# Two-layer decoder trunk: the first weights in halves, one queue for the first columns of x, later transposes in TensorE's order

## The chip, the cores and the metric

The kernel runs on one core of a Trainium2 chip. The metric is device time in microseconds (us) from start to end of one launch. Before the change, three runs took 282.30, 281.93 and 282.25 us; the median is 282.25 us. A profiled execution of the same program took 281.82 us; the first to the last instruction of it span 280.0 us.

Engines are named as in the profile: PE is TensorE's matmul stream, PEld its weight loads, DVE is VectorE, ACT ScalarE, POOL GpSimd, SP SyncE. SP computes nothing here: it issues nearly all DMAs, in the order of its program, and waits where one of them must wait.

## The reference, cut to what matters

Sequence 256, model width 1024, two layers, heads of 64. Each layer projects the normalised rows to ten column blocks, runs three kinds of attention on them, gates each with silu, and multiplies by one output matrix. A last norm follows.

```python
for layer in range(DEPTH):
    h = rms_norm(x, norm_g[layer])
    proj = jnp.einsum('btd,dc->btc', h, w_in[layer])
    sb_q, sb_k, sb_v, sb_g, mb_q, mb_k, mb_v, mb_g, mem_q, mem_g = jnp.split(proj, split_at, axis=-1)
    o_sb = stick_breaking_attention(...)          # 6 heads, causal, in log space
    o_sb = merge_heads(o_sb) * jax.nn.silu(sb_g)
    o_mb = moba_attention(q_mb, k_mb, ...)        # 6 heads, rotary, causal softmax (one block here)
    o_mb = merge_heads(o_mb) * jax.nn.silu(mb_g)
    m = rms_norm(mem, mem_norm_g[layer])
    mk, mv = jnp.split(jnp.einsum('bmd,dc->bmc', m, w_mem_kv[layer]), 2, axis=-1)
    o_mem = memory_attention(..., mk, mv)         # 4 heads, softmax over 256 memory tokens
    o_mem = merge_heads(o_mem) * jax.nn.silu(mem_g)
    mixed = jnp.concatenate([o_sb, o_mb, o_mem], axis=-1)
    x = x + jnp.einsum('btc,cd->btd', mixed, w_out[layer])
return rms_norm(x, final_norm_g)
```

## The kernel before, in words

**Products in three passes.** Each factor of a projection is split into a rounded part (hi) and the rest (lo); TensorE computes hi times hi, hi times lo and lo times hi. For weights, a transfer brings a chunk of 384 KB (128 partitions by 768 numbers) into one of five buffers `raw`; ScalarE or VectorE casts it to hi (tile `hl`, line 245 or 266), VectorE subtracts to get lo (line 251). There are seven `hl` buffers, so the weights can run some chunks ahead of TensorE. When VectorE has finished the lo of a chunk, its `raw` buffer is free and SP issues the load of the chunk five places later. A chunk holds as many of the eight slices of the contraction (k = 0 to 7, called rows of weights here) as fit into 768 columns.

**The start.** Layer 0 begins with `sb_qk`: 768 columns, so one chunk is one row of weights. Row k needs the transposed input x^T of that row too (tile `uT`, 128 KB a row), which ScalarE scales to hi and VectorE to lo (tile `T`, lines 247 and 255). The first row of weights comes as two chunks of 384 columns, the others as one each. ACT's queue issues the two halves of row 0 and row 1 of x^T, SP's queue the rest. Six banks of PSUM accumulate the six blocks of 128 columns side by side; row 0 is computed first for banks 1 to 3 (first half of the weights) and then for banks 4 to 6.

**The order of the work.** All engines get their instructions in an order that the program works out while it is built: tasks (generators) ask for an engine, for marks that must be set, and for buffers; the class `Sched` keeps a clock for each engine from estimated costs, and at each step takes the request that can start first, with priorities among those that can start at nearly the same time. The large projections are one task, `main`, with the lowest priority; scores, transposes and products with values are tasks that slip in between. The pieces of weights are loaded and multiplied in the order of the table `ORDER`. TensorE's order is fixed once the program is built: an instruction whose data is late holds up all behind it.

**Between the layers.** When the output projection of layer 0 ends, the norm of layer 1 is computed for two tiles of 128 rows: squares, logarithm and exponential on ScalarE, two products of 512 columns per tile on VectorE (tile `w`, line 255), four transposes for each on TensorE (line 234, from `w` and the identity in `cst`), and hi and lo of the result into `T` (lines 245 and 251). TensorE has the memory projections `mk` and `mv` of layer 1 to do at that time; they don't need the norm.

**Turns through memory.** The softmax weights of a pair of heads and the rotated keys are transposed in blocks on VectorE (tile `D`), written to memory and read back in another order (tile `Z`): two DMAs one after the other, for which the planner counts a latency `TRIP_LAT` each on top of its transfer time.

Lines that the steps of the prediction touch: the costs and places in lines 27 to 52, `_avail` (119 to 141), the cutting into chunks (370 to 385), `hi_task` (404 to 411), the first loads (436 to 444), `norm_task` (570 to 592), `soft_head` (709 to 734), and the loop of `sb_qk` in `main` (from line 1050).

Of the kernel before, what the change touches and what calls it, by code (L numbers as in the profile page):

```python
# [27 lines left out]
RAW = 5  # L28
KORD = (0, 1, 2, 3, 4, 5, 6, 7)
LAT_SAME, LAT_CROSS = 130.0, 240.0  # L30
P_H0 = -8
P_RX = 1
P_M0 = 12
P_RM = 12
P_M1 = 4
URG = 2
X67_AT = 6
CST_AT = 7
X0_AT = 9
X1_AT = 12  # L40
DMA_GBS = 380.0
SP_ISSUE = 450.0
DMA_LAT = 2200.0
DMA_GBS_1K = 300.0
TRIP_LAT = 4000.0
MEM_FIRST = (False, False)
MEM_AT = 1
ORDER = (["sb_qk", "mem_q", "mb_k", "mb_q", "mk", "mv", "sb_v", "sb_g", "mb_g", "mb_v", "mem_g"],
         ["mk", "mv", "sb_g", "mb_k", "mb_q", "mb_g", "mem_g", "sb_q", "mem_q", "sb_k", "sb_v", "mb_v"])
GATES = {"sb_g": ((0, 1, 2),), "mb_g": ((0, 1, 2),), "mem_g": ((0,), (1,))}  # L50
HOLD = 4000.0
SPARE2 = 2
DVE_HI = 400.0
# [27 lines left out]
class Sched:  # L81
# [37 lines left out]
    def _avail(self, k, eng):  # L119
        r = k.req  # L120
        t = k.t
        if k.eng == eng:
            t += 0.0 if eng == "pe" else LAT_SAME
        elif k.eng:
            t += LAT_CROSS
        for n in r.get("need", ()):
            if n not in self.ready:
                return None
            t = max(t, self.ready[n])
        for tag in r.get("alloc", ()):  # L130
            items = self.res[tag].items
            spare = r.get("spare", 0)
            if "form" in r and r["form"] == self.form:
                spare = r.get("spare2", spare)
            if len(items) <= spare:
                return None
            t = max(t, self.res[tag].best()[0])
        cond = r.get("cond")
        if cond is not None and not cond():
            return None  # L140
        return t

    def _by_form(self, cands):

# [54 lines left out]
def hybrid_trunk(ctx: ExitStack, tc: tile.TileContext, x, mem, norm_g, w_in, w_mem_kv, w_out,  # L199
                 final_norm_g, xT, memT, gcols, consts, out):  # L200
    nc = tc.nc
# [67 lines left out]
    def R(*eng, **kw):  # L269
        kw["eng"] = [e if isinstance(e, tuple) else (e, 0.0) for e in eng]  # L270
        return kw
# [81 lines left out]
    for l in range(DEPTH):  # L353
# [4 lines left out]
        for n in names:  # L358
            if n in COLS:
                c, w = COLS[n]  # L360
                order.append(Piece(n, l, wi[:, :, c:c + w], w))
            elif n[:2] == "wo":
                c = 384 * int(n[2])
                w = min(384, D - c)
# [5 lines left out]
    chunks = []  # L370
    for p in order:
        i = 0
        while i < KT:
            kk = [p.kord[i]]
            i += 1
            while i < KT and len(kk) < p.nk and p.kord[i] == kk[-1] + 1:
                kk.append(p.kord[i])
                i += 1
            half = p.width // 2 if not chunks else p.width
            for c in range(0, p.width, half):  # L380
                for n, k in enumerate(kk):
                    p.kmap.setdefault(k, []).append((c, len(chunks), n * half))
                chunks.append((p, kk, c, half))
# [20 lines left out]
    def hi_task():  # L404
        for j, (p, kk, _, w) in enumerate(chunks):
            w = len(kk) * w
            e, _ = yield R(*([] if j == 0 else [("act", 0.833 * w)]), ("dve", 0.52 * w + DVE_HI), 
                           need=[("raw", j)] + ([("free", j - LEAD)] if j >= LEAD else []))
            copy(his[j % LEAD][:, :w], raws[j % RAW][:, :w], e)
            S.mark(("hi", j))  # L410
            prog["hi"] = j + 1
# [24 lines left out]
    dma_chunk(q=nc.scalar)  # L436
    load_xT(0, 1)
    dma_chunk(q=nc.scalar)
    load_xT(1, 2, nc.scalar)
    for k in range(2, 4):  # L440
        dma_chunk()
        load_xT(k, k + 1)
    dma_chunk()
    load_xT(4, 6)

    def bcast_row(vec, name):
# [123 lines left out]
    def norm_task(l, t, H, done):  # L570
        src = xs[:, t, :]
        r = ss[l, t][:, 7:8]
        yield from rstd(ss[l, t], 3, r)
        for q in range(2):
            s = slice(q * 512, (q + 1) * 512)
            _, (w,) = yield R("dve", need=[("gb", 0)], alloc=["w"])
            stt(w, src[:, s], r, gb[:, s], OP.mult, OP.mult)
            _, (pt,) = yield R("pe", alloc=["bank"])
            for i in range(4):
                tr(pt[:, i * 128:(i + 1) * 128], w[:, i * 128:(i + 1) * 128], ident)  # L580
            S.free("w", w)
            pv = pt.rearrange("p (k c) -> p k c", k=4)
            o_hi = H[0][:, q * 4:q * 4 + 4, t * 128:(t + 1) * 128]
            o_lo = H[1][:, q * 4:q * 4 + 4, t * 128:(t + 1) * 128]
            yield R("act")
            act(o_hi, pv)
            yield R("dve")
            tt(o_lo, pv, o_hi.bitcast(F32), OP.subtract)
            S.free("bank", pt)
            S.mark(done + (q,))  # L590
        S.mark(done)
# [22 lines left out]


    wTs, scs, sps, ws, Fs, ropes = {}, {}, {}, {}, {}, {}
    turn = {"sb": 0, "w": 0}
    HCOL = {"sb": 0, "mb": 384, "mem": 768}
    VN = {"sb": "sb_v", "mb": "mb_v", "mem": "mv"}

# [14 lines left out]
    def pair_scores(l, kind, c):  # L635
# [20 lines left out]
        if kind != "mem":  # L656
            yield R("pe")
            for h in range(2):
                for j, o in enumerate((slice(0, 128), slice(256, 384))):
                    if kind == "sb":  # L660
                        mm(sc[h][:, o], masks[:, 0, :], identb, False, j == 1)
                    else:
                        mm(sc[h][:, o], identb, masks[:, 1, :], False, j == 1)
        for h in range(2):
            S.mark(("qkdone", l, kind, 2 * c + h))
            scs[l, kind, 2 * c + h] = sc[h]
# [41 lines left out]

    def soft_head(l, h, kind):
        mb = kind == "mb"  # L710
        first = (2 if mb else 0) if MEM_FIRST[l] else (0 if mb else 3)
        reg = [(0, 128), (128, 384)] if mb else [(0, 256), (256, 512)]
        _, (st,) = yield R("dve", alloc=["st"], need=[("qkdone", l, kind, h)])
        sc = scs.pop((l, kind, h))
        for t, (r0, r1) in enumerate(reg):
            nc.vector.tensor_reduce(st[:, t:t + 1], sc[:, r0:r1], axis=AX.X, op=OP.max, negate=True)  # L716
            S.op("dve", 1.0417 * (r1 - r0) + 65.0)
            if t == 0:
                yield R("dve")
        _, (w,) = yield R("act", alloc=["w"], cond=lambda: 5 * l + first + h // 2 <= turn["w"] + 1)  # L720
        for t, (r0, r1) in enumerate(reg):
            act(w[:, r0:r1], sc[:, r0:r1], AF.Exp, bias=st[:, t:t + 1], accum_out=st[:, 2 + t:3 + t])
        S.free("bank", sc)
        yield R("dve")
        nc.vector.reciprocal(st[:, 0:2], st[:, 2:4])
        S.op("dve", 81.0)
        yield R("dve")
        for t, (r0, r1) in enumerate(reg):
            ts(w[:, r0:r1], w[:, r0:r1], st[:, t:t + 1])
        S.free("st", st)  # L730
        S.mark(("w", l, kind, h))
        ws[l, kind, h] = w
# [244 lines left out]
    def main():  # L977
# [26 lines left out]
        for l in range(DEPTH):  # L1004
# [45 lines left out]
            if l == 0:  # L1050
# [3 lines left out]
                    accs.append((yield from bank()))  # L1054
                for k in range(KT):
                    if k < 4:
                        groups = [range(3), range(3, 6)] if k == 0 else [range(6)]
                        for g in groups:
                            j, o = p.loc(k, g[0] * 128)
                            o -= g[0] * 128  # L1060
# [129 lines left out]
```

## Time and profile before

| | us |
|---|---|
| runs | 282.30, 281.93, 282.25 (median 282.25) |
| profiled execution | 281.82 |
| its span | 280.0 |
| PE busy | 270.7 (97% of the span) |
| PEld busy | 242.7 (87%) |
| DVE busy | 229.9 (82%) |
| ACT busy | 185.0 (66%) |
| POOL busy | 3.9 (1%) |
| mean granted TensorE clock | 0.998 of full speed |

An engine's busy time is the time covered by its instructions. PE's records overlap, since matmuls are pipelined, so a PE that is always busy need not run at its peak; what the tables of waits show is time in which no record covers PE. An instruction is listed with the tile it writes, an arrow, and the tiles it reads; "T<-uT,gc" is a slice of x^T being scaled.

### The profile page before, as it was taken

How to read it: one execution, taken by the hardware profiler on the slowest of the kernel's cores; microseconds unless marked ns; L12 is line 12 of the kernel's file. 1: busy time of each engine (PE TensorE's matmuls, PEld its weight loads, DVE VectorE, ACT ScalarE, POOL GpSimd, SP SyncE). 2: the span in 40 equal slices, each digit the busy share in tenths (PEclk: the TensorE clock that was granted, in tenths of full speed). 3: DMA queues.
4: the chain of work that ended last, by engine and by line, in shares of the span. 5: the costliest groups of instructions: out<-in, count | busy, mean ns of one | idle time of the engine just before them, and what ended most of it. 6: DMA issues, size and time to landing. Idle time of an engine off the chain costs nothing.

```text
span 280.0 us, 4979 instructions
## 1 busy us (share of the span) xinstructions
PE 270.7 (97%) x1713; PEld 242.7 (87%) x1713; DVE 229.9 (82%) x514; ACT 185.0 (66%) x414; POOL 3.9 (1%) x10
## 2 busy tenths in 40 slices
PE   7899999999999999999999999999999999999991
PEld 4788999898888898898978899988888898988991
DVE  3789899998999999995889489739999999994273
ACT  3879799984696787771866384648974898433053
POOL 0030000010000000000000000000000000000000
PEclk9999999999999999999999999999999999999999
DMA  6999938697588998885476846857358988890004
GB/s 218 348 385 367 367 103 259 188 246 285 165 267 212 263 314 250 242 210 167 129 248 199 272 147 208 250 167 218 104 148 290 248 265 219 263 248 14 0 0 150
DMA packets 45720, 60.49 MB, mean 216 GB/s; under 512 B 3328, under 2 KB 42368, under 8 KB 45696
## 3 DMA queue, kind: packets, MB, share of 16 engines
q1 hardware_dynamic: 44688, 58.22, 67.7%
q0 software_dynamic: 288, 1.05, 1.5%
q10 hardware_dynamic: 720, 0.92, 1.0%
q8 instruction: 13, 0.21, 0.3%
q14 instruction: 11, 0.09, 0.1%
HBM read 53.89 MB, written 6.29 MB: 215 GB/s over the span
## 4 chain that ended last, share of the span: by engine, by line
PE 91%; DMA 4%; ACT 2%; DVE 2%; issue 1%; ACTq 0%; DVEq 0%
PE bank L229 90%; DMA uT<-xT_dram 2%; DMA raw<-in_w_in_dram 2%; PE bank L234 1%; DVE hl L251 1%; ACT hl L245 1%; DVE xs L251 0%; ACT junk L247 0%; DVE w L255 0%; ACT rn L247 0%; ACT ss L247 0%; ACT T L247 0%; ACT T L245 0%; ACTq L332 0%; ACT L206 0%
## 5 line engine op out<-in xcount | busy, mean ns | idle before, releaser
L251 DVE TENSOR_TENSOR hl<-raw,hl 128x768 fp32r<-128x768 f32 (+2 forms) x111 | 101.2, 919 | 8.8 <-ACT hl L245 7.3
L229 PE MATMUL bank<-T,hl 128*128 128x512 f32 (+1 forms) x582 | 106.6, 340 | 1.6 <-ACT hl L245 1.1
L229 PEld LDWEIGHTS bank<-T,hl 128*128 128x128 f32 x582 | 89.2, 190 | 15.7 <-ACT hl L245 1.3
L245 ACT CAST hl<-raw 128x768 fp32r<-128x768 f32 (+2 forms) x100 | 79.4, 808 | 21.2 <-PE bank L229 16.1
L229 PE MATMUL bank<-hl,T 128*128 128x384 f32 (+1 forms) x448 | 82.0, 337 | 0.0
L229 PEld LDWEIGHTS bank<-hl,T 128*128 128x128 f32 x448 | 76.4, 188 | 1.6 <-issue 0.2
L229 PE MATMUL bank<-hl,mxhi 128*128 128x384 f32 (+1 forms) x192 | 45.3, 319 | 0.0
L229 PEld LDWEIGHTS bank<-hl,mxhi 128*128 128x128 f32 x192 | 33.3, 189 | 1.5 <-issue 1.5
L229 PE MATMUL bank<-hl,mxlo 128*128 128x384 f32 (+1 forms) x96 | 30.4, 317 | 0.0
L247 ACT ACTIVATE junk<-xs 128x384 bf16<-128x384 f32 (+2 forms) x16 | 8.4, 523 | 21.6 <-DVE xs L251 20.8
L247 ACT ACTIVATE w<-bank,st 128x256 f32<-128x256 f32 (+1 forms) x40 | 17.3, 447 | 5.2 <-DVE st L716 4.2
L229 PEld LDWEIGHTS bank<-hl,mxlo 128*128 128x128 f32 x96 | 18.1, 189 | 0.0
L247 ACT ACTIVATE ga<-ga 128x768 f32<-128x768 f32 (+1 forms) x24 | 14.9, 628 | 1.6 <-DVE ga L255 1.3
L247 ACT ACTIVATE T<-uT,gc 128x256 fp32r<-128x256 f32 x24 | 11.2, 500 | 5.2 <-DMA uT<-xT_dram 5.2
L245 ACT COPY gT<-bank 128x256 f32<-128x256 f32 x16 | 5.9, 372 | 12.3 <-PE bank L229 12.2
L251 DVE TENSOR_TENSOR xs<-bank,xs 128x384 f32<-128x384 f32 (+1 forms) x12 | 6.1, 510 | 9.3 <-PE bank L229 9.3
L255 DVE SCALAR_TENSOR_TENSOR T<-uT,gc,T 128x256 fp32r<-128x256 f32 x24 | 11.3, 479 | 2.8 <-ACT T L247 2.8
L251 DVE TENSOR_TENSOR gT<-bank,gT 128x256 f32<-128x256 f32 x16 | 6.7, 418 | 7.9 <-ACT gT L245 7.8
L716 DVE TENSOR_REDUCE st<-bank 128x1 f32<-128x256 f32 (+1 forms) x40 | 13.0, 367 | 0.0
L746 DVE STREAM_TRANSPOSE D<-w 128x384 f32<-128x384 f32 (+1 forms) x20 | 12.2, 617 | 0.0
L247 ACT ACTIVATE a<-a 128x384 f32<-128x384 f32 x24 | 11.9, 529 | 0.0
L259 DVE TENSOR_SCALAR w<-w,st 128x256 f32<-128x256 f32 (+1 forms) x40 | 11.0, 320 | 0.0
(112 smaller groups left out, 251.8 us busy)
## 6 DMA issues: line engine op xcount, KB each, us to landing
raw<-in_w_in_dram SPq DMA_DIRECT2D x71, 384.0 KB, 4.7
raw<-in_w_out_dram SPq DMA_DIRECT2D x20, 384.0 KB, 4.4
raw<-in_w_mem_kv_dram SPq DMA_DIRECT2D x8, 384.0 KB, 3.3
Z<-D SPq DMA_DIRECT2D x8, 384.0 KB, 4.7
T<-Z SPq DMA_DIRECT2D x24, 96.0 KB, 5.1
uT<-memT_dram SPq DMA_DIRECT2D x8, 256.0 KB, 5.5
Z<-D SPq DMA_DIRECT2D x4, 512.0 KB, 5.2
T<-Z SPq DMA_DIRECT2D x16, 128.0 KB, 5.0
```

Source lines behind the costliest of these rows:

```text
L229: nc.tensor.matmul(out, lhsT=lhsT, rhs=rhs, start=start, stop=stop, **kw)
L234: nc.tensor.transpose(out, in_, idt)
L245: nc.scalar.copy(out, in_)
L247: nc.scalar.activation(out, in_, func, **kw)
L251: nc.vector.tensor_tensor(out, a, b, op=op)
L255: nc.vector.scalar_tensor_tensor(out, a, s, b, op0=op0, op1=op1)
L259: nc.vector.tensor_scalar(out, a, s, None, op0=op)
L716: nc.vector.tensor_reduce(st[:, t:t + 1], sc[:, r0:r1], axis=AX.X, op=OP.max, negate=True)
L746: nc.vector.transpose(o, w[:, :n * 128].rearrange("p (m j r) -> p m j r", j=4, r=32))
```

## The change

Six things change; all but the first two act through the planner.

- The halves of a row: the first four chunks, not the first two, are half a row, so row 1 comes as two transfers of 192 KB. In TensorE's order row 1 is computed as row 0 is, first for banks 1 to 3, then for 4 to 6. The hi of the third chunk is VectorE's alone.
- The first loads: row 1 of x^T moves from ACT's queue to SP's, behind row 0 of x^T and ahead of the weights of row 1; rows 2 and 3 of x^T stand behind the chunks of rows 1 and 2. The places of the loads of x (`X0_AT`, `X1_AT`) and of the last rows of x^T (`X67_AT`) are counted in chunks and move with them.
- A request for TensorE by any task but `main` counts as able to start 100 ns later (`PE_LATE`), and the transposes of the norm 1200 ns later (`NORM_LATE`).
- `TRIP_LAT` is 3500 instead of 4000 ns.
- `ORDER`: in layer 0 `mb_k` stands before `mem_q` and `mv` before `mk`; in layer 1 `sb_g` moves from behind `mv` to behind `sb_k`, and `mb_g` stands before `mb_q`.
- The turn in which softmax heads may take a buffer `w` follows the order in which their scores were computed (`place`), not a fixed table.

```diff
+PE_LATE = 100.0
+NORM_LATE = 1200.0
-X67_AT = 6
+X67_AT = 7
-X0_AT = 9
-X1_AT = 12
+X0_AT = 8
+X1_AT = 13
-TRIP_LAT = 4000.0
-MEM_FIRST = (False, False)
+TRIP_LAT = 3500.0
-ORDER = (["sb_qk", "mem_q", "mb_k", "mb_q", "mk", "mv", "sb_v", "sb_g", "mb_g", "mb_v", "mem_g"],
-         ["mk", "mv", "sb_g", "mb_k", "mb_q", "mb_g", "mem_g", "sb_q", "mem_q", "sb_k", "sb_v", "mb_v"])
+ORDER = (["sb_qk", "mb_k", "mem_q", "mb_q", "mv", "mk", "sb_v", "sb_g", "mb_g", "mb_v", "mem_g"],
+         ["mk", "mv", "mb_k", "mb_g", "mb_q", "mem_g", "sb_q", "mem_q", "sb_k", "sb_g", "sb_v", "mb_v"])
...
-        return t
+        return t + r.get("late", PE_LATE) if eng == "pe" and k.gen.__name__ != "main" else t
...
-            half = p.width // 2 if not chunks else p.width
+            half = p.width // 2 if len(chunks) < 4 else p.width
...
-            e, _ = yield R(*([] if j == 0 else [("act", 0.833 * w)]), ("dve", 0.52 * w + DVE_HI), 
+            e, _ = yield R(*([] if j in (0, 2) else [("act", 0.833 * w)]), ("dve", 0.52 * w + DVE_HI), 
...
-    load_xT(1, 2, nc.scalar)
-    for k in range(2, 4):
-        dma_chunk()
-        load_xT(k, k + 1)
+    load_xT(1, 2)
     dma_chunk()
+    dma_chunk()
+    load_xT(2, 3)
+    dma_chunk()
+    load_xT(3, 4)
     load_xT(4, 6)
...
-            _, (pt,) = yield R("pe", alloc=["bank"])
+            _, (pt,) = yield R("pe", alloc=["bank"], late=NORM_LATE)
...
+        if kind != "sb":
+            place[l, kind, c] = len(place)
...
-        _, (w,) = yield R("act", alloc=["w"], cond=lambda: 5 * l + first + h // 2 <= turn["w"] + 1)
+        _, (w,) = yield R("act", alloc=["w"], cond=lambda: place[l, kind, h // 2] <= turn["w"] + 1)
...
-                        groups = [range(3), range(3, 6)] if k == 0 else [range(6)]
+                        groups = [range(3), range(3, 6)] if k < 2 else [range(6)]
```

**The start.** SP's queue from its first load, before (`uT` is x^T, `raw` a buffer for weights, `gc` the gains):

```order
L332 DMA gc_66<-gcols_dram 128x32
L332 DMA uT_73<-xT_dram 128x256
L332 DMA raw2_91<-in_w_in_dram 128x768
L332 DMA uT_73<-xT_dram 128x256
L332 DMA raw3_92<-in_w_in_dram 128x768
L332 DMA uT_73<-xT_dram 128x256
L332 DMA raw4_93<-in_w_in_dram 128x768
L332 DMA uT_73<-xT_dram 128x2x256
L332 DMA raw0_89<-in_w_in_dram 128x768
```

And now:

```order
L333 DMA gc_66<-gcols_dram 128x32
L333 DMA uT_73<-xT_dram 128x256 x2
L333 DMA raw2_91<-in_w_in_dram 128x384
L333 DMA raw3_92<-in_w_in_dram 128x384
L333 DMA uT_73<-xT_dram 128x256
L333 DMA raw4_93<-in_w_in_dram 128x768
L333 DMA uT_73<-xT_dram 128x256
L333 DMA uT_73<-xT_dram 128x2x256
L333 DMA raw0_89<-in_w_in_dram 128x768
```

Row 1 of x^T is the second of the two loads in the second line; the two halves of row 1 of the weights take buffers 2 and 3, row 2 takes buffer 4, and row 3, which stood in buffer 4, now waits for buffer 0.

VectorE from its first cast, before (`hl0` and `hl1` are the halves of row 0, `hl2` is row 1):

```order
L266 CAST hl0_94<-raw0_89 128x384
L251 TENSOR_TENSOR hl0_94<-raw0_89,hl0_94 128x384
L255 SCALAR_TENSOR_TENSOR T0_74<-uT_73,gc_66,T0_74 128x256
L251 TENSOR_TENSOR hl1_95<-raw1_90,hl1_95 128x384
L255 SCALAR_TENSOR_TENSOR T0_74<-uT_73,gc_66,T0_74 128x256
L251 TENSOR_TENSOR hl2_96<-raw2_91,hl2_96 128x768
L255 SCALAR_TENSOR_TENSOR T0_74<-uT_73,gc_66,T0_74 128x256
L251 TENSOR_TENSOR hl3_97<-raw3_92,hl3_97 128x768
```

And now (`hl2` and `hl3` are the halves of row 1, `hl4` is row 2):

```order
L267 CAST hl0_94<-raw0_89 128x384
L252 TENSOR_TENSOR hl0_94<-raw0_89,hl0_94 128x384
L256 SCALAR_TENSOR_TENSOR T0_74<-uT_73,gc_66,T0_74 128x256
L252 TENSOR_TENSOR hl1_95<-raw1_90,hl1_95 128x384
L256 SCALAR_TENSOR_TENSOR T0_74<-uT_73,gc_66,T0_74 128x256
L267 CAST hl2_96<-raw2_91 128x384
L267 CAST hl3_97<-raw3_92 128x384
L252 TENSOR_TENSOR hl2_96<-raw2_91,hl2_96 128x384
L256 SCALAR_TENSOR_TENSOR T0_74<-uT_73,gc_66,T0_74 128x256
L252 TENSOR_TENSOR hl3_97<-raw3_92,hl3_97 128x384
L252 TENSOR_TENSOR hl4_98<-raw4_93,hl4_98 128x768
```

Both casts of row 1 are VectorE's, and the lo of its second half stands behind the lo of row 2 of x^T.

**Between the layers.** TensorE around the second group of transposes of the norm, before (`w3` and `w1` are products of the norm, `T0` and `hl` the factors of `mk`; a line of 128x512 and one of 128x256 are one slice):

```order
L229 MATMUL bank1_102<-T0_74,hl0_94 128x256
L234 MATMUL bank7_108<-cst_65,w3_115 128x128 x4
L229 MATMUL bank1_102<-T0_74,hl0_94 128x512
L229 MATMUL bank1_102<-T0_74,hl0_94 128x256
L234 MATMUL bank3_104<-cst_65,w1_113 128x128 x4
L229 MATMUL bank1_102<-T0_74,hl1_95 128x512
```

And now:

```order
L230 MATMUL bank4_105<-T0_74,hl2_96 128x256
L235 MATMUL bank1_102<-cst_65,w3_115 128x128 x4
L230 MATMUL bank4_105<-T0_74,hl2_96 128x512
L230 MATMUL bank4_105<-T0_74,hl2_96 128x256
L230 MATMUL bank4_105<-T0_74,hl2_96 128x512
L230 MATMUL bank4_105<-T0_74,hl2_96 128x256
L230 MATMUL bank4_105<-T0_74,hl3_97 128x512
```

From the end of the output projection, the four groups of transposes stood behind 4, 20, 22 and 36 matmuls of `mk` and `mv`; they now stand behind 12, 24, 36 and 48 of the 64.

VectorE there, before (`ss00` and `ss01` are the factors of the two tiles of rows):

```order
L255 SCALAR_TENSOR_TENSOR w0_112<-xs_64,ss00_151,gb_72 128x512
L251 TENSOR_TENSOR xs_64<-bank2_103,xs_64 128x256
L251 TENSOR_TENSOR hl4_98<-raw0_89,hl4_98 128x768
L251 TENSOR_TENSOR hl5_99<-raw1_90,hl5_99 128x512
L251 TENSOR_TENSOR T1_75<-bank5_106,T1_75 128x4x128
L255 SCALAR_TENSOR_TENSOR w3_115<-xs_64,ss01_152,gb_72 128x512
L255 SCALAR_TENSOR_TENSOR w1_113<-xs_64,ss00_151,gb_72 128x512
```

And now:

```order
L256 SCALAR_TENSOR_TENSOR w2_114<-xs_64,ss00_151,gb_72 128x512
L252 TENSOR_TENSOR xs_64<-bank2_103,xs_64 128x256
L252 TENSOR_TENSOR hl5_99<-raw1_90,hl5_99 128x768
L252 TENSOR_TENSOR hl6_100<-raw2_91,hl6_100 128x512
L256 SCALAR_TENSOR_TENSOR w3_115<-xs_64,ss01_152,gb_72 128x512
L252 TENSOR_TENSOR hl0_94<-raw3_92,hl0_94 128x768
L252 TENSOR_TENSOR T1_75<-bank0_101,T1_75 128x4x128
L256 SCALAR_TENSOR_TENSOR mem_k_81<-bank5_106,mem_k_81 128x256
L256 SCALAR_TENSOR_TENSOR w0_112<-xs_64,ss00_151,gb_72 128x512
```

The product for the second tile of rows (`w3`) now stands ahead of the lo of the first transposes (`T1`), not behind it.

## Rows read from the trace of the kernel before

**Rows 1.** The page's busy times: us, share of the span, instructions.

```profile
PE 270.7 (97%) x1713; PEld 242.7 (87%) x1713; DVE 229.9 (82%) x514; ACT 185.0 (66%) x414; POOL 3.9 (1%) x10
```

**Rows 2.** Waits of PE, whole span: total us, times, longest us.

```profile
PE bank L229 <- ACT hl L245: 1.1, 1, 1.1
PE bank L234 <- DVE w L255: 0.6, 1, 0.6
PE bank L229 <- ACT T L247: 0.4, 1, 0.4
PE bank L229 <- ACT rn L247: 0.2, 1, 0.2
```

**Rows 3.** Timeline of PE, 3 to 9 us: start, us, what, [idle before].

```profile
4.72 2.85 PE L229 MATMUL bank<-T,hl 128*128 128x256 f32 x18 [0.37 <-ACT T L247]
8.67 0.50 PE L229 MATMUL bank<-T,hl 128*128 128x512 f32 x1 [1.10 <-ACT hl L245]
```

**Rows 4.** Timeline of ACT, 0 to 13 us.

```profile
7.39 0.51 ACT L247 ACTIVATE T<-uT,gc 128x256 fp32r<-128x256 f32 x1 [2.32 <-DMA uT<-xT_dram]
7.80 0.81 ACT L245 CAST hl<-raw 128x768 fp32r<-128x768 f32 x1
```

**Rows 5.** Timeline of DVE, 0 to 13 us.

```profile
3.27 0.36 DVE L266 CAST hl<-raw 128x384 fp32r<-128x384 f32 x1 [2.13 <-DMA raw<-in_w_in_dram]
3.66 0.56 DVE L251 TENSOR_TENSOR hl<-raw,hl 128x384 fp32r<-128x384 f32 x1
...
7.93 0.49 DVE L255 SCALAR_TENSOR_TENSOR T<-uT,gc,T 128x256 fp32r<-128x256 f32 x1 [2.27 <-ACT T L247]
```

**Rows 6.** Timeline of SP, 0 to 10 us (DMA issues).

```profile
1.19 0.42 SPq L332 DMA_DIRECT2D uT<-xT_dram  x1
1.65 0.42 SPq L332 DMA_DIRECT2D raw<-in_w_in_dram  x1
...
4.09 0.33 SPq L332 DMA_DIRECT2D raw<-in_w_in_dram  x1
```

**Rows 7.** DMA issues from 1.3 to 1.5 us (first row) and 1.8 to 2.0 us: KB, us to landing.

```profile
uT<-xT_dram SPq DMA_DIRECT2D x1, 128.0 KB, 2.9
...
raw<-in_w_in_dram SPq DMA_DIRECT2D x1, 384.0 KB, 5.5
uT<-xT_dram ACTq DMA_DIRECT2D x1, 128.0 KB, 5.7
```

**Rows 8.** Timeline of PE, 139.5 to 151 us.

```profile
140.12 0.88 PE L229 MATMUL bank<-T,hl 128*128 128x512 f32 x4
...
141.19 3.07 PE L229 MATMUL bank<-T,hl 128*128 128x512 f32 x16
144.86 0.66 PE L234 MATMUL bank<-cst,w 128*128 128x128 f32 x4 [0.61 <-DVE w L255]
```

**Rows 9.** Timeline of ACT, 139 to 151 us.

```profile
142.86 0.57 ACT L245 CAST T<-bank 128x512 fp32r<-128x512 f32 x1
143.32 0.53 ACT L247 ACTIVATE ss<-ss 128x1 f32<-128x1 f32 x2
```

**Rows 10.** Chain of work that ended last, 133 to 150 us: start, us, what.

```profile
146.31 2.45 PE bank L229 x14
148.75 0.44 PE bank L234 x4
```

**Rows 11.** DVE by line, 133 to 150 us: count, busy us, mean ns, idle before.

```profile
L251 DVE TENSOR_TENSOR hl<-raw,hl 128x768 fp32r<-128x768 f32 (+1 forms) x9 | 7.6, 858 | 0.0
L255 DVE SCALAR_TENSOR_TENSOR w<-xs,ss,gb 128x512 f32<-128x512 f32 x4 | 2.9, 746 | 0.9 <-ACT ss L247 0.9
L251 DVE TENSOR_TENSOR T<-bank,T 128x512 fp32r<-128x512 f32 x4 | 2.7, 685 | 1.0 <-ACT T L245 1.0
...
L255 DVE SCALAR_TENSOR_TENSOR mem_k<-bank,mem_k 128x256 f32<-128x256 f32 x2 | 0.8, 415 | 0.0
```

**Rows 12.** Tile `Z`, all its DMAs (60).

```profile
DMA to landing us min/median/max: 2.2/5.1/7.2
```

More of the change, by code (lines that the diff above doesn't have):

```diff
@@ L616, in hybrid_trunk @@
     wTs, scs, sps, ws, Fs, ropes = {}, {}, {}, {}, {}, {}
-    turn = {"sb": 0, "w": 0}
+    turn, place = {"sb": 0, "w": 0}, {}
     HCOL = {"sb": 0, "mb": 384, "mem": 768}
@@ L710, in soft_head @@
         mb = kind == "mb"
-        first = (2 if mb else 0) if MEM_FIRST[l] else (0 if mb else 3)
         reg = [(0, 128), (128, 384)] if mb else [(0, 256), (256, 512)]
```

## The prediction

> **What bounds the kernel now.** I began with the page's busy times: PE covers 97% of the span, DVE 82%, ACT 66% [rows 1]. The number of matmuls doesn't change (1585 in the program before and after), so the change can only move time in which TensorE stands still, at its start, its end or between. The waits of PE say how much there is [rows 2]: 1.1 us for the cast of a weight chunk, 0.6 us for a product of the norm, 0.4 us for the first slice of x^T and 0.2 us for a bank: 2.3 us in all. The 0.4 us belongs to row 0, whose loads stay as they are. So at most 1.9 us is to be had from waits, unless the new order is better in ways that these rows don't hold.
>
> Next I placed the waits. PE's timeline at the start has 18 matmuls of row 0 from 4.72 to 7.57 us, and the first of row 1 at 8.67 us, after 1.10 us for the cast by ACT [rows 3]. That cast began at 7.80 us, behind the scaling of row 1 of x^T, which began at 7.39 us when its transfer landed [rows 4]. The second is between the layers: PE does 4 matmuls of `mk`, transposes, 16 more, and then stands 0.61 us at 144.86 us until the norm's next product is there [rows 8]. The third, 0.2 us for a bank, is in layer 0.
>
> **The start.** Removed: one cast of 768 columns on ACT (0.81 us [rows 4]) and one issue on ACT's queue. Added: two casts of 384 columns on DVE (0.36 us each) and two subtractions of 384 (0.56 us each) for one of 768 [rows 5], and two issues on SP (0.42 us each [rows 6]): row 1 of x^T goes out at 1.65 us, the halves of the weights at about 2.1 and 2.6 us.
>
> When do they land? Row 0 of x^T, issued at 1.19 us, took 2.9 us, so it landed at 4.1 us; row 1 of x^T and its weights, issued at 1.65 and 1.68 us, took 5.7 and 5.5 us and landed at 7.4 and 7.2 us [rows 6, 7]. That is 512 KB in 3.3 us, 157 KB per us, with others under way beside it. At this pace, and in the new order, the 128 KB of x^T land at 4.9 us, the first half of the weights (192 KB) at 6.1 us and the second at 7.4 us. The bounds for x^T are 4.5 us (2.9 us after its issue, as row 0) and 7.4 us (5.7 us after, as before).
>
> From there by DVE's order: x^T is scaled on ACT (0.51 us) and DVE (0.49 us) by 6.0 us; the cast of the first half ends at 6.1 + 0.4 = 6.5 us. TensorE comes free at 7.57 us and doesn't wait. Now a matmul takes 0.175 us in the mean of 512 and 256 columns (2.45 us for 14 [rows 10]), so three pairs, half a row, take 1.05 us, and a row 2.1 us. The cast of the second half ends at 7.8 us, the lo of the first at 8.3 us; TensorE wants it after three long matmuls, at 8.3 us. The lo of the second half stands behind the scaling of row 2 of x^T, which lands at some 7.6 us at least: 7.6 + 0.5 + 0.5 = 8.6 us, then 0.56 us, 9.2 us; TensorE wants it at 9.3 us. That is tight, and may cost 0.1 us.
>
> Row 3 pays for the halves: it was the fifth chunk, issued at 4.09 us [rows 6], and is now the sixth, whose SP instruction waits, in the built program, for the semaphore that the first half of row 1 sets, so 6.1 us. With 4.5 to 5.5 us to land (the spread around rows 7) and 0.81 us of cast it is ready between 11.4 and 12.4 us; TensorE reaches row 3 at 7.57 + 4.2 = 11.8 us. That gives back 0 to 0.6 us. SP's instructions behind it (row 4, x, the constants) wait as long; TensorE needs row 4 2.1 us later, so its cover is larger. The start gives -1.1 + 0.1 + 0.1 = -0.9 us; the bounds are -1.1 and -0.3 us.
>
> **Between the layers.** The four groups of transposes stood behind 4, 20, 22 and 36 matmuls of `mk` and `mv`, and now behind 12, 24, 36 and 48. From 140.12 us [rows 8], with 2.1 us for 12 matmuls and 0.44 us for a group of transposes [rows 10], they come at 142.2, 144.8, 147.3 and 149.8 us. The product for the first had begun before 140.12 us. The second (`w3`) hung on ACT: its factor came from the two small activations at 143.32 us, behind the cast of the first transposes at 142.86 us [rows 9]. In ACT's new order they stand ahead of that cast, so they end 0.46 us earlier, at 143.4 us, and DVE makes `w3` next (0.75 us [rows 11]): 144.1 us, 0.7 us before TensorE wants it. The third then follows a lo (0.86), the lo of the first transposes (0.69) and a piece of `mk` (0.42) with its own 0.75 us [rows 11]: 146.9 us, for 147.3 us. The fourth has the same four in front: 149.6 us, for 149.8 us. Behind the last group are 16 matmuls of `mv` (2.8 us) and the first four slices of `mb_k`, which need only the first halves of the norm; the last lo isn't missed. So the 0.6 us go; I count -0.65 us, since the weight load waited too. The bounds are -0.65 and 0 us: the margins of 0.4 and 0.2 us are within what one late chunk would take.
>
> **The rest.** The bank wait [rows 2] hung on an evacuation of `mb_q` that now lies beside another piece: between -0.2 and 0, I take -0.1 us. `ORDER`, `PE_LATE`, `TRIP_LAT` and `place` move work without adding any; what they may add is waits of the same kind. The order before left 0.8 us of these in the 271 us after the start [rows 2]. A new order by the same planner may hold as many in new places: 0 to 0.8 us, I take 0.2 us, since the two known ones are counted above. `sb_g` of layer 1, moved to behind `sb_k`, takes its gate to a later place, but `sb_v` and `mb_v`, 96 matmuls, follow it before the output projection.
>
> Sum: -0.9 - 0.65 - 0.1 + 0.2 = -1.45 us. The profiled execution took 281.82 us (span 280.0 us and 1.8 us around it), so 280.4 us. It lies 0.43 us under the median of the runs; on that scale I predict 282.25 - 1.45 = 280.8 us.
>
> **The rivals.** First, that the queue changes nothing. In the trace, row 1 of x^T on ACT's queue and its weights on SP's landed 0.2 us apart [rows 6, 7], as if they shared the engines. If x^T comes no sooner on SP's queue than 5.7 us after its issue, it lands at 7.35 us, is scaled at 7.9 and 8.4 us, and row 1 starts at 8.4 instead of 8.67 us: only 0.3 us gained, and the sum is -0.3 - 0.65 - 0.1 + 0.2 = -0.85 us: 281.4 us. Against it: row 0 of x^T took 2.9 us on SP's queue [rows 7], and in the new order row 1 is the very next in that queue. The Trainium skill (DMA: Bandwidth & Descriptors, Issuing engines are not separate DMA queues) says that DMAs of all issuing engines interleave on the same engines, and that another issuer saves the issue time alone. The landings 0.2 us apart agree with the interleaving; by that sentence alone the move would be worth nothing or cost SP one issue.
>
> Second, that everything is covered and the new order leaves no waits: -1.1 - 0.65 - 0.2 = -1.95 us, 280.3 us. For it speak the margins at the start except two; against it that a planner that misjudged two places before will do so again.
>
> Third, slower: the turns through memory come late. `TRIP_LAT` is 500 ns shorter, so the planner thinks the data of scores and values to be back up to 1.0 us sooner (two DMAs) and sets TensorE's stretches of scores and values accordingly; TensorE stands at the first that comes too soon, and all projections behind it stand too. The 60 DMAs took 2.2 to 7.2 us, 5.1 us in the median [rows 12]; the planner counts 2.2 + 3.5 us and 1.0 us for 384 KB, 6.7 us, so only the slowest fall out of it, by 0.5 us. There are six stretches that hang on a turn (keys, `mb` values and `mem` values in each layer); if each cost 0.5 us and the start gave back its 0.9 us, the sum would be +3.0 - 0.65 - 0.1 = +2.3 us. Half of that, +1.15 us, makes 283.4 us. It decides from about 1.7 us of such waits on, that is, three to four stretches. No wait for a turn stands in the table of PE's waits [rows 2], and the median leaves 1.6 us.
>
> **How the numbers follow.** The forecast has 0.5 (its own range 280.1 to 281.5 us), the unchanged queue 0.2, all covered 0.18, late turns 0.12. The range reaches up over the first rival and part of the third, and down a little below the second, since the order may be better where I see nothing: 279.5 to 282.7 us. A change under 0.2% (0.56 us) can't be told from none here. Faster than 281.69 us are the forecast, all covered, and half and a bit of the first rival: 0.78. Between 281.69 and 282.81 us lie the rest of it and a mild third: 0.12. Slower: 0.10.
>
> **What would show it.** Right: PE starts row 1 before 7.8 us, ACT's wait for row 1 of x^T ends before 5.5 us, the second group of transposes has no wait, and PE's waits for `hl` and `w` are under 0.5 us together. The first rival shows as row 1 of x^T landing past 7 us. The halves cost more than I think if PE waits again around 11.8 us for row 3. The third shows as PE waits released by a DMA of `T<-Z` or `uT<-Z`. It would be wrong altogether if PE's waits fell by 1.5 us and the time didn't: then the end or the pace of TensorE moved.

## The result and the profile after

The changed kernel takes 279.69 us (median of 11 runs, 278.92 to 281.47) where the kernel before takes 282.25 us (11 runs, 280.78 to 283.54). The ratio is 0.9926 with a 95% interval of [0.9901, 0.9951]: faster by 0.74%, some 2.1 us (the ratio is of the means; the two medians stand 2.56 us apart). The prediction was 280.8 us, a gain of 1.45 us, with a range from 279.5 to 282.7 us. The profiled execution took 279.69 us and spans 277.9 us.

The page's first line, busy time by engine, answers to [rows 1]; TensorE's work is the same, the span is shorter:

```profile
PE 270.2 (97%) x1713; PEld 242.5 (87%) x1713; DVE 230.6 (83%) x517; ACT 184.2 (66%) x413; POOL 3.6 (1%) x10
```

PE's waits (total us, times, longest us) answer to [rows 2]. The one for `junk`, at the very start, is in both kernels:

```profile
PE bank L230 <- DVE junk L983: 1.2, 1, 1.2
PE bank L230 <- ACT T L248: 0.4, 1, 0.4
PE bank L235 <- DVE w L256: 0.3, 1, 0.3
```

The waits for `hl` (1.1 us) and for a bank (0.2 us) are gone, that for the norm's product `w` fell from 0.6 to 0.3 us, and none came in their place: 1.6 us less of waits.

At the start, the DMA issues of 1.6 to 1.7 us and of 2.0 to 2.7 us (KB each, median us to landing) answer to [rows 7], and ACT's and DVE's timelines to [rows 4, 5]:

```profile
uT<-xT_dram SPq DMA_DIRECT2D x1, 128.0 KB, 3.0
...
raw<-in_w_in_dram SPq DMA_DIRECT2D x2, 192.0 KB, 4.7
```

```profile
5.03 0.51 ACT L248 ACTIVATE T<-uT,gc 128x256 fp32r<-128x256 f32 x1
```

```profile
6.87 0.84 DVE L267 CAST hl<-raw 128x384 fp32r<-128x384 f32 x2 [0.76 <-DMA raw<-in_w_in_dram]
```

Row 1 of x^T went out at 1.65 us as before and landed 3.0 us later instead of 5.7, so ACT scales it at 5.03 us instead of 7.39. Both halves of row 1's weights are cast by 7.7 us. PE's timeline from 3 to 14 us, which answers to [rows 3], is one unbroken row from row 0 on; the first product of 512 columns, which opens row 1, starts in it at 7.71 us:

```profile
4.78 9.44 PE L230 MATMUL bank<-T,hl 128*128 128x256 f32 x54 [0.42 <-ACT T L248]
```

Between the layers, PE's timeline answers to [rows 8]. The transposes stand behind 12, 12, 12 and 12 more products; the second group still waits:

```profile
138.46 2.29 PE L230 MATMUL bank<-T,hl 128*128 128x512 f32 x12
140.59 0.60 PE L235 MATMUL bank<-cst,w 128*128 128x128 f32 x4
140.94 2.35 PE L230 MATMUL bank<-T,hl 128*128 128x512 f32 x12
143.62 0.66 PE L235 MATMUL bank<-cst,w 128*128 128x128 f32 x4 [0.33 <-DVE w L256]
```

The chain of work that ended last, around that wait (start, us, what), tells why:

```profile
135.44 5.45 DMA raw<-in_w_in_dram
...
140.97 0.84 ACT hl L246
141.81 0.42 ACT junk L248 x2
142.23 0.02 issue
142.25 0.30 ACT ss L248
...
142.82 0.76 DVE w L256
143.58 0.04 issue
143.62 0.66 PE bank L235 x4
```

The statistics of the second tile stand on ACT behind the cast of a weight chunk, and that chunk took 5.45 us to land.

For the rest, three stretches of equal work can be told apart in every trace by the starts of three products: the first of row 1 (512 columns wide), the first of layer 1's `mk`, and the last of all. The table gives each stretch in us, read from these starts, and two things that the experiments turned on: how many of row 0's 18 products took 200 ns or more to the next start, and the time (median) with its ratio to runs of the kernel before on the same chip. The stretches are of one execution each, and not always of a typical one: the start alone was profiled in the second slowest of its twelve runs, all but the start in the fastest of its twelve.

| kernel | slow in row 0 | to row 1 | row 1 to `mk` | `mk` to last | median | ratio, 95% |
|---|---|---|---|---|---|---|
| before | 4 | 8.67 | 131.45 | 133.71 | 282.25 | |
| changed | 6 | 7.71 | 130.75 | 133.44 | 279.69 | 0.9926 [0.9901, 0.9951] |
| changed, on another chip | 18 | 8.92 | 130.85 | 132.91 | 279.88 | 0.9921 [0.9891, 0.9952] |
| start alone | 18 | 9.15 | 131.84 | 134.47 | 281.78 | 0.9996 [0.9973, 1.002] |
| all but the start | 4 | 8.06 | 131.33 | 132.91 | 281.42 | 0.9985 [0.997, 1.0001] |
| changed, x^T row 1 on ACT | 6 | 8.33 | 130.78 | 133.23 | 279.41 | 0.9919 [0.9901, 0.9937] |
| changed, norm not late | 18 | 8.90 | 131.05 | 133.57 | 280.76 | 0.9967 [0.9948, 0.9986] |
| changed, five zeros | 15 | 8.21 | 130.69 | 132.90 | 280.41 | 0.9947 [0.9928, 0.9967] |
| before, nine zeros | 1 | 8.76 | 130.97 | 133.28 | 281.18 | 0.9947 [0.9929, 0.9966] |
| start alone, nine zeros | 3 | 7.50 | 131.95 | 133.81 | 280.98 | 0.9937 [0.9918, 0.9956] |
| all but the start, nine zeros | 9 | 8.02 | 131.33 | 132.91 | 281.24 | 0.9941 [0.9921, 0.9961] |
| old `ORDER`, nine zeros | 6 | 7.75 | 131.31 | 133.50 | 280.39 | 0.9943 [0.992, 0.9966] |
| x^T row 1 on ACT, nine zeros | 2 | 8.48 | 130.86 | 132.91 | 279.76 | 0.9918 [0.989, 0.9946] |
| changed, nine zeros | 2 | 7.52 | 130.70 | 132.93 | 279.05 | 0.9872 [0.985, 0.9893] |

From before to changed that is -0.96, -0.70 and -0.27 us; the other 0.20 us of the 2.13 between the profiled executions lie behind the last product (7.99 and 7.79 us to the end), where the engines do the same work and the last transfers land sooner. That was not followed up.

### The profile page after: what moved, and what is told of

Read it like the earlier page. It is cut to its first block, busy times and chain, and to the rows that moved or that the text cites. A ratio compares the mean times of both kernels' runs of the same rounds, so it can differ in the third digit from the quotient of the medians.

```text
span 277.9 us, 4990 instructions
## 1 busy us (share of the span) xinstructions
PE 270.2 (97%) x1713; PEld 242.5 (87%) x1713; DVE 230.6 (83%) x517; ACT 184.2 (66%) x413; POOL 3.6 (1%) x10
## 4 chain that ended last, share of the span: by engine, by line
PE 92%; DMA 3%; DVE 2%; ACT 1%; issue 0%; SPq 0%; DVEq 0%; ACTq 0%
PE bank L230 91%; DMA raw<-in_w_in_dram 2%; DMA uT<-xT_dram 1%; PE bank L235 1%; DVE hl L252 1%; DVE xs L252 0%; ACT ss L248 0%; ACT junk L248 0%; ACT hl L246 0%; DVE w L256 0%; ACT T L248 0%; SPq L333 0%; DVE ss L527 0%; DVE xs L260 0%; DVEq L1189 0%
## 5 line engine op out<-in xcount | busy, mean ns | idle before, releaser
L246 ACT CAST hl<-raw 128x768 fp32r<-128x768 f32 (+2 forms) x101 | 80.5, 811 | 23.2 <-PE bank L230 7.6
```

Source lines behind the costliest of these rows:

```text
L246: nc.scalar.copy(out, in_)
```

## The experiments

The kernel before ran beside each group of four: 281.86 us in the median with the first four, 283.0 with the second, 281.96 with the third, on different chips.

**The start alone.** The kernel before with the halves, the cast on DVE, the loads and their places:

```diff
-    load_xT(1, 2, nc.scalar)
+    load_xT(1, 2)
...
-            half = p.width // 2 if not chunks else p.width
+            half = p.width // 2 if len(chunks) < 4 else p.width
```

> The kernel before with the changes of its start alone: row 1 of x^T on SyncE's queue, row 1 of the weights in two halves, both cast by VectorE, and the constants' places in the list of loads. Theory (the parts are separate, and the start is worth about 1.0 us of the 2.1 measured between the two kernels): row 1 starts at 7.7 to 7.8 us with no wait for hl, x^T row 1 lands before 5 us, the norm's wait of about 0.6 us stays, and the time is 0.30 to 0.45% under the kernel before (281.0 to 281.4 us on the scale of 282.25). Rival (the gain needs the new order too, because what TensorE gains at the start it loses at the next wait of layer 0): row 1 starts early but the last matmul of layer 0 stands within 0.4 us of its old place, and the time is within 0.15% of the kernel before.

Measured: no gain (281.78 us, ratio 0.9996). The wait for `hl` is gone, that for the norm is 1.0 us. The theory fell. Its trace shows two reasons. The first is in PE's timeline from 3 to 9 us, beside [rows 3]:

```profile
5.14 4.18 PE L229 MATMUL bank<-T,hl 128*128 128x256 f32 x18 [0.79 <-ACT T L247]
```

The same 18 products took 4.18 us here and 2.85 us in the kernel before. After the first, their starts stand 213 to 214 ns apart to the last one, which for 256 columns is 1.2 GHz. In the kernel before that holds up to the fourth, and the others stand 113 to 121 ns apart, the upper level (2.4 GHz would be 107 ns). The second reason is that the planner set layer 0 anew: from row 1 to `mk` it took 0.39 us more than before, and the norm's wait grew.

**All but the start.** The changed kernel with the start of the one before (the diff above, backwards).

> The changed kernel with the start of the one before: row 1 of the weights whole and cast by ScalarE, row 1 of x^T on ScalarE's queue; the new order, the late norm transposes, the turn's time and the softmax weights' order stay. Theory (the remainder is worth 0.9 to 1.1 us, most of it in layer 0 and not between the layers): a wait of about 1.1 us for hl before row 1 is back, the norm's wait is 0.2 to 0.4 us, the time is 0.3 to 0.4% under the kernel before (281.1 to 281.4 us on its scale). Rival (the prediction's own terms, where the remainder was worth 0.65 + 0.1 - 0.2 = 0.55 us): 0.2% under, 281.7 us.

Measured: 281.42 us, 0.15% under, interval up to 1.0001. That is nearer to the rival's 0.2% than to the theory's 0.3 to 0.4%: the remainder alone is worth 0.4 us, with an interval from nothing to 0.85 us. The wait for `hl` is 0.4 us here and not 1.1, because the same loads landed sooner in this run (x^T row 1 after 5.1 us, not 5.7). The two halves of the change, which bring 2.1 us together, bring 0.1 and 0.4 us alone.

**Row 1 of x^T on ACT's queue again.**

```diff
-    load_xT(1, 2)
+    load_xT(1, 2, nc.scalar)
```

> The changed kernel with one load put back: row 1 of x^T is issued on ScalarE's queue again, behind the second half of row 0's weights; the halves of row 1's weights stay on SyncE's. Theory (the queue's order counts: what stands behind 192 KB of weights in its queue lands after them): x^T row 1 lands at 6 us or later, its scaling ends past 6.5 us, and the first matmul of row 1 is at 8.0 us or later, with a wait on T of 0.3 us or more. Rival (queues share the engines evenly and another issuer saves the issue alone): it lands within 0.5 us of the 4.65 us of the changed kernel, row 1 starts at 7.7 us without a wait, and the time is that of the changed kernel.

The issue of that load (KB, us to landing):

```profile
uT<-xT_dram ACTq DMA_DIRECT2D x1, 128.0 KB, 5.2
```

It lands at 6.87 us, row 1 starts at 8.33 us after a wait of 0.9 us: the mechanism is the theory's (the wait is listed for `hl`, since VectorE's casts of row 1 stand behind its part of that scaling). The time is that of the changed kernel all the same (0.9919 beside 0.9926). What the queue is worth shows only with nine zeros, further down.

**The norm not late.** `NORM_LATE` is 100 in the changed kernel.

```diff
-NORM_LATE = 1200.0
+NORM_LATE = 100.0
```

> The changed kernel with the norm's transposes at their old urgency (late by 100 ns, as other work, not by 1200): they stand behind 6, 22, 22 and 40 matmuls of the second layer's first projections instead of 12, 24, 36 and 48. Theory (their place sets the wait): waits on w of 0.6 to 1.2 us are back between the layers, 0.3 to 0.9 us more than the 0.33 us of the changed kernel, and the time is 0.1 to 0.3% above it. Rival (what sets that wait is the late weight chunk in front of the norm's statistics on ScalarE, so the place moves only where TensorE waits): the waits for w and hl between the layers add up to 0.2 to 0.5 us and the time is that of the changed kernel within 0.1%.

Measured: 280.76 us, 0.4% more than the changed kernel by the two ratios, whose intervals just overlap; in the profiled run all of row 0 ran at the low level. The listed wait for `w` is 0.24 us, as the rival has it, yet from `mk` to the last product it takes 133.57 us beside 132.91:

```profile
144.66 1.32 PE L235 MATMUL bank<-cst,w 128*128 128x128 f32 x8 [0.24 <-DVE w L256]
145.74 1.99 PE L230 MATMUL bank<-T,hl 128*128 128x512 f32 x10
```

From 144.66 to 145.74 us are 1.08 us for two groups of transposes; a group otherwise takes 0.35 us to the next product. So 0.38 us of waiting lie between the records and are in no table of waits: together 0.62 us, close to the 0.66 us. No late chunk is behind it: here the chunk in front of the statistics landed 1.15 us after the first `mk`, sooner than in the trace with 132.91 us (1.67 us).

**Nine matmuls of zeros.** All kernels begin with seven matmuls of zeros, which end at 4.15 us (one starts every 0.43 us); then TensorE stands until row 0 of x^T has been scaled. Four kernels got nine, with the rest of TensorE's order unchanged:

```diff
-        for _ in range(7):
+        for _ in range(9):
             mm(acc, junk[:, :128], junk, True, True)
```

The kernel before:

> The kernel before with nine matmuls of zeros ahead of row 0 instead of seven (0.43 us each, so they end at about 5.0 us and not at 4.15), all else equal. Theory (TensorE's clock level at the start hangs on whether it stands still between those and row 0: 256 columns take 213 ns at 1.2 GHz and 120 at 2.4; in the profiled runs so far the low pace held for 4 to 18 of row 0's 18 matmuls, longest where the pause was longest): with no pause the low pace ends before 6 us, in four matmuls or fewer; row 0 starts 0.1 to 0.3 us later; the time is 0 to 0.3% under the kernel before (281.1 to 281.9 us on the scale of 281.9), with its upper runs gone. Rival (the low pace is a fixed time after the first product of row 0, or comes from the data): as many slow matmuls as before or more, and the time is 0.1 to 0.2% over it.

Measured: 281.18 us where the kernel before has 283.0 us on this chip, 0.53% less, and seven runs within 1.1 us. The theory had 0.3% at most; on this chip the kernel before takes some 1 us more than on the other two, for a reason that stays open, so ratios from different chips compare only roughly. One slow product is left in row 0.

The changed kernel:

> The changed kernel with nine matmuls of zeros instead of seven. Theory: the six slow matmuls of its profiled run become four or fewer, row 1 starts by 7.8 us in spite of a later row 0, and the time is 0.1 to 0.3% under the changed kernel: 278.9 to 279.4 us. Rival (the pause has no part in it): 0.1% over it, 279.9 us.

Measured: 279.05 us, runs from 278.89 to 279.54. Its only wait is the one for the zeros:

```profile
PE bank L230 <- DVE junk L983: 1.2, 1, 1.2
```

Two products of row 0 take 200 ns or more instead of six, and row 1 starts at 7.52 us although row 0 starts 0.33 us later.

The start alone:

> The kernel before with the start's changes alone and nine matmuls of zeros. Theory (the start alone came out at no gain because in its profiled run all 18 matmuls of row 0 ran at the low pace, 1.3 us, and because the attention's small matmuls took 0.84 us more in its order): the 1.3 us are gone, the 0.84 stay, and the time is 0.2 to 0.5% under the kernel before: 280.5 to 281.3 us. Rival (what is gained at the start is lost to later waits whatever the clock): within 0.15% of the kernel before, 281.4 to 282.3 us.

Measured: 280.98 us, in the theory's bounds; but beside 281.18 us for the kernel before with nine zeros that is only 0.2 us. The start gives 1.26 us until row 1; 0.98 us go back in layer 0, and 0.53 us behind it. Where in layer 0, PE's timeline shows at 62 to 76 us, first of the kernel before with nine zeros:

```profile
65.64 1.14 PE L229 MATMUL bank<-mem_k,mem_q 64*128 64x256 f32 x8
66.61 1.48 PE L229 MATMUL bank<-uT 64*128 64x128 f32 x16
68.02 0.62 PE L229 MATMUL bank<-masks,identb 128*128 128x128 bf16 x8
...
73.55 1.12 PE L229 MATMUL bank<-mem_k,mem_q 64*128 64x256 f32 x8
```

and of the start alone:

```profile
65.17 1.58 PE L229 MATMUL bank<-uT 64*128 64x128 f32 x16
66.68 0.62 PE L229 MATMUL bank<-masks,identb 128*128 128x128 bf16 x8
...
71.14 1.72 PE L229 MATMUL bank<-mem_k,mem_q 64*128 64x256 f32 x8
72.79 3.39 PE L229 MATMUL bank<-hl,T 128*128 128x384 f32 x18
```

The same eight products of `mem_q` with `mem_k` take 1.72 us where they take 1.14 or 1.12 us: each has 64 rows, and in the short stretches the starts of two lie 6 to 7 or 92 ns apart; here the third waited for ACT (tile `w`), and the pairs came apart. This is not the order's doing alone. In the trace of the kernel before, whose order is that of the kernel with nine zeros, the second eight lost 0.45 us in the same way, the third waiting for ACT's `sb_v`:

```profile
73.49 1.56 PE L229 MATMUL bank<-mem_k,mem_q 64*128 64x256 f32 x8
```

The number of stretches is the order's. Between row 1 and `mk` the products that read no weights lie in 19 stretches here and in 16 in the kernel before with nine zeros; from start to start they take 0.5 us more here, and the projections' products around them the other 0.5 us. The rival's reading (lost in later places) is the right one; in the first experiment's trace the low level of row 0 came on top.

All but the start:

> The changed kernel with the start of the kernel before and nine matmuls of zeros. Theory: this start is seldom late for the clock, so little changes against the same kernel with seven: 281.0 to 281.5 us, 0.1 to 0.3% under the kernel before; and the start's part is worth the difference to the changed kernel with nine, 1.6 to 2.2 us, more than the 1.1 us of the wait that went. Rival (the start's part is worth its wait, 1.1 us, once the clock is out of it): 280.0 to 280.5 us.

Measured: 281.24 us, as the theory has it in time; its 9 slow products in row 0 are more than it allows. Here the small products lie in 20 stretches, and in the changed kernel in 16 again. So with nine zeros the start alone is worth 0.2 us and the remainder nothing, neither of them clear of noise, and both together 2.1 us.

**The changed kernel once more**, to have it on one chip with the last three:

> The changed kernel as it is (seven matmuls of zeros), on the chip of the next three. Theory (the change is worth about 2 us where TensorE's clock level at the start is the same in both, and single runs differ by how long row 0 stays at the low pace): 0.6 to 0.9% under the kernel before, runs spread over 2 us or more. Rival (the gain of 2.1 us was in part the luck of one chip's runs, and the change's own part is the 1.5 us of the prediction): 0.4 to 0.6%.

Measured: 279.88 us, 0.79% under the kernel before: the theory's. This profiled run has 18 slow products, an exact copy of the program with six in the other trace. Two rows show it, each of the view by stretches for the products that read `T` (stretch, us, busy and count, granted clock, DMA share, GB/s); the first is of this run, the second of the changed kernel with nine zeros:

```profile
5.60:6.60 1.00, 1.00 (x7) 1.00 1.01 310
```

```profile
5.60:6.60 1.00, 1.00 (x10) 1.00 0.99 349
```

The granted clock reads 1.00 in both, and PE is covered in both; of what the views print, only the count tells that one runs at the lower level. The traces themselves agree with the count: their records of the granted clock begin, at full clock, at 9.22 us in this run and at 4.84 us in the other, and a view prints 1.00 for time without a record. In this run the norm's second group had no wait: the chunk of weights in front of its statistics landed 1.67 us after the first `mk`, not 2.43 us as in the first trace.

**Five zeros.** The changed kernel with `range(5)`.

> The changed kernel with five matmuls of zeros instead of seven, so that they end at about 3.3 us and TensorE stands still for some 1.5 us before row 0. Theory (the pause sets the clock back): the 256-column matmuls of row 0 all take 213 ns, the low pace ends at about 9 us, and the time is 0.8 to 1.4 us over the changed kernel in nearly every run. Rival (the pace of row 0 has to do with its data, or with chance): as many slow matmuls as with seven, 3 to 8, and the changed kernel's time within 0.3 us.

Measured: 15 slow products and 0.53 us over the changed kernel (280.41 and 279.88 us). The direction is the theory's, though the intervals of the two ratios overlap, and the size is below it: row 0 of x^T came early in this run, row 0 started at 4.47 us and the low level ended at 7.8 us, not at 9.

**Row 1 of x^T on ACT's queue, nine zeros.**

> The changed kernel with row 1 of x^T on ScalarE's queue and nine matmuls of zeros. Theory (the queue's place is worth what row 1 waits): x^T row 1 lands at 6.5 to 7.2 us, row 1 of TensorE starts 0.5 to 0.9 us later than in the changed kernel with nine, and the time is 0.5 to 0.9 us over it, about 0.2 to 0.3% (279.6 to 280.0 us where that has 279.05). Rival (what TensorE loses there it gets back, since the chunks behind are then early): the same time within 0.2 us.

Measured: it lands at 7.02 us, 5.3 us after its issue, while row 0 of x^T on SP's queue took 3.1 us:

```profile
8.48 3.71 PE L230 MATMUL bank<-T,hl 128*128 128x512 f32 x18 [1.01 <-DVE hl L267]
```

Row 1 starts 0.96 us later than in the changed kernel with nine, the last product 1.10 us later. The median of 279.76 us is in the theory's bounds, 0.7 us over the changed kernel with nine, which ran on another chip. So with nine zeros the queue is worth some 0.7 to 1.1 us, and nothing gives it back; with seven, where row 0's level differs from run to run, no difference was measured.

**The old `ORDER`, nine zeros.**

> The changed kernel with the order of projections of the kernel before (the table ORDER alone put back) and nine matmuls of zeros. Theory (with the new start the old order costs the attention's stretches of layer 0 what the start's changes alone showed, 0.8 to 1.2 us more between 14 and 140 us): 0.7 to 1.3 us over the changed kernel with nine, 279.8 to 280.4 us where that has 279.05. Rival (the order is worth nothing by itself; the softmax weights' order or the late norm made the difference): within 0.3 us of it.

Measured: 280.39 us, in the theory's bounds (1.34 us over the changed kernel with nine, on another chip); 0.61 us more from row 1 to `mk`, 0.57 us more behind. The table of the projections' order, which moves work and adds none, is worth 1.2 us after row 1 here.

## Why the prediction was right, and where its terms were off

**The direction and the first term were right for the reason given.** The start was to give 0.9 us; row 1 of TensorE starts 0.96 us earlier in the two profiled executions, and 1.24 us earlier where both have nine zeros. Row 1 of x^T was forecast at 4.9 us and landed at 4.65; the halves at 6.1 and 7.4 us landed at 6.84 and 7.32. The 0.1 us for the lo of the second half and the 0.1 us for row 3 were not spent: row 3's cast ended 0.13 us before TensorE came to it. Of the four signs of being right three came; the second group of transposes waited all the same. Two small slips move nothing: 512 KB in 3.3 us are 155 KB per us, not 157, and the trace counts 1713 matmuls, not 1585, equally many in both kernels.

**The rival on the queue is out.** Issued within 0.04 us of the same time, row 1 of x^T lands 3.0 to 3.6 us after its issue on SP's queue (eight traces) and 5.0 to 5.8 us on ACT's (six). The Trainium skill (DMA: Bandwidth & Descriptors, Issuing engines are not separate DMA queues) says that all issuers' transfers interleave on the same engines and that another issuer saves the issue alone; here the load's place in the two queues was worth 1.4 us of its landing or more, and the measurement decides. What in the hardware makes the difference was not tested.

**Between the layers** the term was -0.65 us and the two profiled executions show -0.27. The mechanism holds: put back alone, the late norm is worth 0.66 us (133.57 and 132.91). What failed is the margin. I had the second product of the norm 0.7 us ahead of TensorE; in the profiled run a weight chunk came late, ACT cast it before the statistics, and the product was 0.33 us behind. The prediction said that one late chunk would take such a margin, and priced none. The 0.61 us that the term removes were in part one trace's, too: with nine zeros the kernel before has no listed wait for `w`, and its stretch behind the first `mk` is 133.28 us, 0.35 us over the changed kernel's 132.93.

**The step that was wrong is the one on the order**: "`ORDER`, `PE_LATE`, `TRIP_LAT` and `place` move work without adding any; what they may add is waits", at +0.2 us, with -0.1 us for the bank. From row 1 to the first `mk` the change took off 0.70 us, and 0.27 us with nine zeros; 0.45 us of the 0.70 are the eight products that came apart in the kernel before's trace. A new order changes how the small products of attention are grouped, and a late operand how they pair, and so how long TensorE takes over them without a listed wait. And the terms don't add: the start alone was worth 0.1 to 0.2 us in time, the rest alone 0.0 to 0.4, both 2.1. The start's term held because it was priced inside the new order, where the gain stays; in the old one nearly all of it went. The sum itself was short by 0.6 us of the 2.1, and that the time fell inside the range is owed to the lower end, drawn "since the order may be better where I see nothing", and not to a term. Which of `place`, `PE_LATE` and `TRIP_LAT` does the part that `ORDER` doesn't was not tried, nor the move of the load without the halves.

**The rival of late turns** shows nowhere: no wait for `T<-Z` or `uT<-Z` stands in any of the tables of PE's waits. "All covered" (280.3 us) was the nearest in time, with 0.33 us of waits left that it didn't have.

**What I did not see** is the level of TensorE's clock in row 0. It was in the kernel before, too (four of 18 products), hidden in a row that I read as "18 matmuls of row 0 from 4.72 to 7.57 us". It moves a run by an estimated 1.3 us (14 more products at 213 instead of 120 ns), which is more than the start's term of 0.9 us.

**A version that beats both** came out of it: the changed kernel with nine zeros, 279.05 us, 0.9872 [0.985, 0.9893] of the kernel before. It and the changed kernel (279.69 and 279.88 us) were not run on one chip.

## What to carry to other kernels

Where a planner or a scheduler fixes the order, a gain at one place isn't a term by itself: what comes earlier there changes the order of all that follows, so price a change together with the order that it is built with, and look at the stretches of small, paired products, whose losses are in no table of waits. A stretch read from one trace can hold half a microsecond that the same program doesn't lose in the next, so read two before a term is taken from it. Count products per microsecond, and don't trust busy time and granted clock alone in the first microseconds, where the clock may not be on record yet. A transfer on which a start hangs goes first in the queue that is short.

## What was not expected of the hardware

Each trace has a record of the moment from which TensorE's clock was granted in full, and the starts of the products change pace at that moment to within 0.1 us. It lies anywhere between 4.4 and 9.7 us. With seven zeros in front and a pause behind them (row 0 at 4.38 to 5.14 us), it was 5.7 to 6.3 us in four traces, with 4 to 6 of row 0's products at the lower level, and 9.2 to 9.7 us in three, with all 18; these are the three with the latest row 0 (4.89, 4.91 and 5.14 us). With five zeros it was 7.9 us. With nine and hardly a pause it was 4.4 to 6.9 us in six traces, and in two of them, the changed kernel and its variant with x^T on ACT's queue, it came while the zeros still ran, so no product of row 0 was at the lower level. So the zeros matter, but whether by closing the pause or by the work that they add was not separated, and they don't set the moment alone (9 slow products in one trace where row 0 followed the zeros at once); what else does stays open.
